# Gated networks of a decoder trunk: two of four weight sums by a transfer that adds, three more block-product pairs in the first network, and another offset for the attention's value weights

## The chip, the cores and the metric

The kernel runs on one core of a Trainium2 chip. The metric is the device time of one execution in microseconds (us), lower is better. It reads HBM through transfers (DMA), works in SBUF, and TensorE (PE) accumulates in PSUM. The other engines are VectorE (DVE), ScalarE (ACT), GpSimd (POOL) and SyncE (SP). Each engine runs its own instructions in order; SP and POOL also issue the transfers here, each in the order of its own queue.

## The reference

Two residual layers over 512 tokens of width 1024 in float32: layer 0 mixes tokens with a state-space block, layer 1 with a forgetting attention of 16 heads, and each is followed by a gated network. Norms are scaled, shifted and gated by adaLN values, which come from products of a conditioning vector with `ada_w`.

```python
def conv_ffn(h, w_up, conv_w, conv_b, w_down):     # h (1, 512, 1024), inner width 2816
    a, b = jnp.split(h @ w_up, 2, axis=-1)
    ap = jnp.pad(a, ((0, 0), (CONV_W - 1, 0), (0, 0)))
    a_conv = conv_b
    for i in range(CONV_W):                        # causal, depthwise, width 3
        a_conv = a_conv + ap[:, i:i + S] * conv_w[i]
    return (jax.nn.silu(a_conv) * b) @ w_down

for i in range(DEPTH):
    h = h + gate * (s5_mixer if i == 0 else fox_mixer)(modulate(h, ...), ...)
    h = h + gate * conv_ffn(modulate(h, ...), ...)
return rmsnorm(h, final_g)
```

## The kernel before

Channels lie on the 128 partitions, the 512 tokens along the free dimension. Every product in question is done in three matmuls: a weight tile and an input are split into a high part (rounded, made by ACT, `w_hi`) and a low part (the rest, made by DVE, `w_lo`), and high x high, high x low and low x high are accumulated (`mms`, L294; `put_parts`, L277 and L278).

**The two networks** (`ffn`). The inner width is 22 tiles of 128. Tile f has a pair of up products, the branch `a` that is convolved and the branch `b` that multiplies it. Inner tiles come in groups: 4, 4, 5, 4, 5 in the first network, 6, 5, 6, 5 in the second. While the pairs of one group are computed, the eight output tiles of the down product of the group before are spread over them, one or two per pair; each is a weight tile of 4 or 5 (second network 5 or 6) blocks of 128 columns. In the first network these down weights are loaded into `rawd`, a room with one buffer, so the second of two tiles can't be loaded until ACT and DVE have read the first. In the second they use `raw`.

**A plain pair** takes two loads of 512 KB (`raw`, three buffers), their parts, and 2 x 8 x 3 matmuls of 512 columns (L294).

**A block-product pair** (`quarters`) takes seven products instead of eight of 4 x 3 matmuls of 256 columns (L550). The weights a11, a12 (branch `a`, upper and lower half of the 1024 inputs), a21, a22 (branch `b`) are combined in four sums s1 to s4 on DVE (L518, tiles `sums`), the inputs in four forms t1 to t4, once per network (`forms_x`, L495). The products are brought together by four combinations on DVE (L518, `nm_t`) from copies that ACT makes of PSUM (L557, `nm_h`). `finish` (`gated`) then makes the two taps (L602) and the gating (L605, L612) and splits the result into `ghi` and `glo`. The list `plain` names the tiles that stay plain; before, 0, 1, 2, 3, 6, 11 and 17 in the first network and 0 to 3 in the second.

**AdaLN sums.** In the first network each tick (one per gated pair after the first group, one after each pair's share of the down product) runs one unit of `ada_units`: DVE multiplies a 512 KB tile with a row and sums it (L247), then POOL's queue loads the next tile into the one buffer `ada_raw` (L233).

**The value weights** of the attention (`fox_values`) are the moving operand of L1366, and lie `VALUES` elements behind the start of their tiles. `aside` does the same for weights of 256-column matmuls, with 22 elements (88 bytes). `fill` only takes up memory.

What each engine does in which order is set by a scheduler that moves instructions of the program by its own estimates; `issue_after` and `behind` restrain it.

Of the kernel before, what the change touches and what calls it, by code (L numbers as in the profile page):

```python
# [8 lines left out]
F32 = mybir.dt.float32  # L9
F32R = mybir.dt.float32r  # L10
I32 = mybir.dt.int32
AF = mybir.ActivationFunctionType
# [5 lines left out]
P = 128  # L18
# [40 lines left out]
def fill(pool, n):  # L59

    pool.tile([P, n // 4], F32, name="fill", bufs=1)


ROOM, ASIDE, VALUES = 9 * P, 22, P - 22


def part_of(pool, shape, name, tag, bufs, aside=0):
# [6 lines left out]
class Trunk:  # L74
# [6 lines left out]
    def __init__(self, tc, io, ctx):  # L81
        self.tc, self.nc, self.io, self.ctx = tc, tc.nc, io, ctx
        nc = self.nc
        pool = lambda name, bufs, **k: ctx.enter_context(tc.tile_pool(name=name, bufs=bufs, **k))
        self.const = pool("const", 1)
        self.act = pool("act", 1)
        self.wpool = pool("wpool", 3)
        self.tmp = pool("tmp", 2)
        self.small = pool("small", 2)
        self.dram = pool("dram", 1, space=DRAM)  # L90
        self.mm = pool("mm", 4, space=PSUM)
        self.aux = pool("aux", 4, space=PSUM)
# [6 lines left out]
        self.room = None  # L99
        self.one = self.const.tile([P, 1], F32, name="one")  # L100
# [11 lines left out]
        fill(self.const, 1728)  # L112
        fill(self.small, 1440 - 1024)

    def load_pack(self, name, parts, pool):
# [360 lines left out]
    def forms_x(self, pool, x):  # L476

        nc = self.nc
        H, N = KT // 2, S // 2
        t1, t2 = HALVES  # L480
        normed = self.last_lo.ins
        b = []
        for j, n in enumerate(("ghi1", "glo1")):
            t = pool.tile([P, H, S], F32, name=f"x{j}", tag=n)
            for c in HALVES:
                k = slice(j * H, (j + 1) * H)
                with self.tc.issue_after(normed):
# [5 lines left out]
        def form(n, u, v):  # L493
            t = pool.tile([P, H, N], F32, name="sums", bufs=2)
            nc.vector.tensor_tensor(t, u, v, ALU.subtract)  # L495
            hi, lo = (pool.tile([P, H, N], F32R, name=m, bufs=4) for m in ("w_hi", "w_lo"))
            self.put_parts(hi, lo, t)
            self.tx[n] = hi, lo
            return t

        f1 = form(1, b[0][:, :, t2], b[0][:, :, t1])
        yield
        f2 = form(2, b[1][:, :, t2], f1)
        yield
        form(4, f2, b[1][:, :, t1])
        yield
        form(3, b[1][:, :, t2], b[0][:, :, t2])
        yield

    def quarters(self, pool, l, f, x, finish):  # L510

        nc = self.nc
        H, N = KT // 2, S // 2
        t1, t2 = HALVES
        a, b = (self.raw([P, KT, P], self.io["w_up"][l][2 * f + j]) for j in range(2))
        a11, a12, a21, a22 = a[:, :H], a[:, H:], b[:, :H], b[:, H:]
        c, d = (pool.tile([P, 2, H, P], F32, name="sums", bufs=2) for _ in range(2))
        sub = lambda o, u, v, op=ALU.subtract: nc.vector.tensor_tensor(o, u, v, op)  # L518
        w = {}
        copied = self.copied  # L520

        def parts(src, names, *where):
            hi, lo = (
                pool.tile([P, H * P + P], F32R, name=n, tag="e" + n)[:, ASIDE:ASIDE + H * P].rearrange("p (n w) -> p n w", w=P)
                if where else part_of(self.wpool, [P, len(names) * H, P], n, n, WB, ASIDE)
                for n in ("w_hi", "w_lo")
            )
            with self.behind(*copied):
                self.put_parts(hi, lo, src)
            for j, n in enumerate(names):  # L530
                w[n] = hi[:, j * H:(j + 1) * H], lo[:, j * H:(j + 1) * H]

        parts(a, ("a11", "a12"))
        sub(c[:, 0], a21, a22, ALU.add)
        sub(c[:, 1], c[:, 0], a11)
        parts(c.rearrange("p n k m -> p (n k) m"), ("s1", "s2"))
        sub(d[:, 1], a11, a21)
        sub(d[:, 0], a12, c[:, 1])
        parts(d.rearrange("p n k m -> p (n k) m"), ("s4", "s3"))
        parts(a22, ("a22",), pool)  # L540
        quarter = lambda k, t: tuple(v[:, k * H:(k + 1) * H, t] for v in x)
        xs = {"b11": quarter(0, t1), "b21": quarter(1, t1), "b22": quarter(1, t2)}
        for n, v in self.tx.items():
            xs[f"t{n}"] = v

        def times(o, wn, xn, first=True):
            (whi, wlo), (xhi, xlo) = w[wn], xs[xn]
            for k in range(H):
                for n, (wt, xt) in enumerate(((whi, xhi), (whi, xlo), (wlo, xhi))):
                    self.last_mm = nc.tensor.matmul(  # L550
                        o, wt[:, k], xt[:, k], start=(first and k == 0 and n == 0), stop=(k == H - 1 and n == 2),
                        skip_group_check=True,
                    )

        def copy(o, last=False):
            t = self.tmp.tile([P, N], F32, name="nm_h", bufs=4)
            a = nc.scalar.activation(t, o, AF.Copy)  # L557
            if last:
                self.copied = [a.ins]
            return t  # L560

        p1, p5 = (self.mm.tile([P, S], F32, name="mmp")[:, :N] for _ in range(2))
        p2, p4 = (self.aux.tile([P, S], F32, name="aux")[:, :N] for _ in range(2))
        oa, ob = (self.tmp.tile([P, S], F32, name="nm_t") for _ in range(2))
        times(p1, "a11", "b11")
        c1 = copy(p1)
        times(p5, "s1", "t1")
        c5 = copy(p5)
        times(p2, "a12", "b21")
        sub(oa[:, t1], p2, c1, ALU.add)  # L570
        times(p1, "s2", "t2", False)
        c2 = copy(p1, True)
        times(p5, "s4", "b22", False)
        sub(oa[:, t2], p5, c2, ALU.add)
        finish(2 * f, oa, slice(0, S))
        times(p4, "a22", "t4")
        c4 = copy(p4)
        times(p1, "s3", "t3", False)
        sub(ob[:, t2], p1, c5, ALU.add)
        sub(ob[:, t1], p1, c4)  # L580
        finish(2 * f + 1, ob, slice(0, S))

    def ffn(self, i, l, x, nxt, ticks=0, plain=None):

        nc, tc = self.nc, self.tc
        with tc.tile_pool(name=f"ffn{l}", bufs=1, reuse_waits="tile") as pool:
            self.bgpool = pool
            conv = pool.tile([P, 4, FT], F32, name="conv_wb")
            nc.sync.dma_start(conv, self.io["conv"][l])
            fill(pool, 1696)  # L590
# [41 lines left out]
            for q, n in enumerate(groups):  # L632
                fs = range(first[q], first[q + 1])
                if not plain:
# [45 lines left out]
class Ew:  # L680
# [29 lines left out]
    def sub(self, a, b, out=None):  # L710
        return self.tt(a, b, ALU.subtract, out)
# [827 lines left out]
def build(tc, io, out, stop=None):  # L1539
    with ExitStack() as ctx:  # L1540
# [105 lines left out]
```

## Time and profile before

| | |
|---|---|
| median of 3 runs | 1214.21 us (1213.31 to 1214.53) |
| profiled execution | 1217.02 us, of which the span of the profile is 1215.2 us |
| clock granted to TensorE, mean | 0.995 |
| DMA | 183.81 MB in 74512 packets, mean 151 GB/s |
| SP's queue / POOL's queue | 161.02 MB, 40.5% / 20.97 MB, 5.4% of 16 engines' span |

All durations below come from the one profiled execution, in us from the start of its span. A row of a group reads: line, engine, operation, output<-inputs, shapes, count, busy us, mean ns of one, and idle time before them with what ended it. A row of the timeline: start, duration, engine, line, operation, count, and in brackets how long the engine had been idle and for whom. A row of a stretch: its limits, its length, then for each engine named the busy time and the number of instructions, the clock granted, the share of the DMA engines and GB/s. A row of waits: who waited for whom, us in total, times, longest. Successive instructions of an engine overlap by some tens of ns, so the distance of starts is what one costs. The lines of the changed kernel are shifted: L277 and L278 become L279 and L280, L518 becomes L533, L550 becomes L563, L602 becomes L614.

### The profile page before, as it was taken

The page shows a single profiled execution, that of the slowest core. Times are in us where ns is not written, and L with a number is a line of the kernel's source. Part 1 is how long each engine was busy: PE and PEld are TensorE (multiplying, and loading weights), DVE is VectorE, ACT ScalarE, POOL GpSimd, SP SyncE. Part 2 cuts the span into 40 slices and gives each one's busy share as a digit, 9 for nine tenths or more (in the row PEclk, how much of TensorE's full clock was granted, in tenths as well). Part 3 has the DMA queues.
Part 4 walks back from the last instruction along what each step waited for, and adds up shares of the span by engine and source line. Part 5 has one row for each costly group of instructions (what it writes and reads, how often), then busy time and mean ns, then how long its engine had stood idle before and what let it go on. Part 6 is the DMA issues. An engine that isn't in the chain of part 4 may idle for free.

```text
span 1215.2 us, 20334 instructions
## 1 busy us (share of the span) xinstructions
PE 1180.3 (97%) x7793; PEld 1015.4 (84%) x7793; DVE 1007.6 (83%) x1872; ACT 609.8 (50%) x1156; POOL 83.9 (7%) x145
## 2 busy tenths in 40 slices
PE   7999999999999999999999999999999999999997
PEld 2566688898989899889899777878989999999987
DVE  7999977789899988898687578875899887888965
ACT  3644555336445454455443565654466554555543
POOL 0000000100000000000000333430000000000000
PEclk9999999999999999999999999999999999999999
DMA  9778786622455544553445543432213332333331
GB/s 348 243 250 261 233 294 220 210 77 70 136 179 164 189 155 148 169 168 106 126 153 180 172 153 130 148 108 88 89 53 113 112 119 90 103 104 109 109 100 70
DMA packets 74512, 183.81 MB, mean 151 GB/s; under 512 B 23231, under 2 KB 25631, under 8 KB 73391
## 3 DMA queue, kind: packets, MB, share of 16 engines
q1 hardware_dynamic: 68367, 161.02, 40.5%
q0 software_dynamic: 5760, 20.97, 5.4%
q8 instruction: 61, 1.00, 0.3%
q10 hardware_dynamic: 288, 0.52, 0.1%
q14 instruction: 36, 0.29, 0.1%
HBM read 175.57 MB, written 6.92 MB: 150 GB/s over the span
## 4 chain that ended last, share of the span: by engine, by line
PE 56%; issue 26%; DVE 8%; DMA 5%; ACT 2%; POOL 2%; SPq 0%; POOLq 0%; DVEq 0%; ACTq 0%
PE mmp L294 24%; PE mmp L550 11%; PE aux L550 4%; PE mmp L1366 3%; PE mmp L1174 2%; DVE w_lo L278 2%; PE mmp L1203 2%; POOL ada_raw L233 1%; PE aux L1505 1%; DMA ada_raw<-in_ada_t 1%; PE aux L1065 1%; PE mmp L1114 1%; PE aux L1057 1%; PE aux L978 1%; DMA yt<-s_yd 1%
## 5 line engine op out<-in xcount | busy, mean ns | idle before, releaser
L278 DVE TENSOR_TENSOR w_lo<-raw,w_hi 128x1024 fp32r<-128x1024 f32 (+4 forms) x173 | 183.3, 1064 | 37.6 <-ACT w_hi L277 31.8
L277 ACT ACTIVATE w_hi<-raw 128x1024 fp32r<-128x1024 f32 (+4 forms) x173 | 154.8, 904 | 105.4 <-PE mmp L294 48.6
L294 PE MATMUL mmp<-ghi,w_hi 128*128 128x512 f32 (+1 forms) x392 | 145.5, 371 | 0.0
L294 PE MATMUL mmp<-ghi,w_lo 128*128 128x512 f32 (+1 forms) x392 | 144.7, 369 | 0.7 <-DVE w_lo L278 0.6
L294 PE MATMUL mmp<-glo,w_hi 128*128 128x512 f32 (+1 forms) x392 | 145.1, 370 | 0.0
L294 PE MATMUL mmp<-a_hi,w_hi 128*128 128x512 f32 (+1 forms) x376 | 138.4, 371 | 1.5 <-ACT a_hi L433 1.5
L294 PE MATMUL mmp<-a_hi,w_lo 128*128 128x512 f32 (+1 forms) x376 | 136.2, 363 | 0.2 <-DVE w_lo L278 0.2
L294 PE MATMUL mmp<-a_lo,w_hi 128*128 128x512 f32 (+1 forms) x376 | 135.7, 362 | 0.0
L550 PE MATMUL mmp<-w_hi 128*128 128x256 f32 x396 | 109.7, 277 | 2.7 <-ACT nm_h L557 2.3
L550 PE MATMUL mmp<-w_hi,w_lo 128*128 128x256 f32 x396 | 109.5, 277 | 0.7 <-DVE w_lo L278 0.7
L550 PE MATMUL mmp<-w_lo,w_hi 128*128 128x256 f32 x396 | 109.4, 276 | 0.0
L557 ACT ACTIVATE nm_h<-mmp 128x256 f32<-128x256 f32 x99 | 37.2, 381 | 107.3 <-PE mmp L550 107.3
L278 DVE TENSOR_TENSOR w_lo<-sums,w_hi 128x1024 fp32r<-128x1024 f32 x74 | 90.0, 1219 | 0.0
L277 ACT ACTIVATE w_hi<-sums 128x1024 fp32r<-128x1024 f32 x74 | 77.0, 1055 | 23.7 <-DVE sums L518 21.7
L294 PEld LDWEIGHTS mmp<-ghi,w_lo 128*128 128x128 f32 x392 | 74.7, 190 | 13.8 <-DVE w_lo L278 1.5
L294 PEld LDWEIGHTS mmp<-ghi,w_hi 128*128 128x128 f32 x392 | 74.7, 191 | 11.5 <-ACT w_hi L277 0.2
L294 PEld LDWEIGHTS mmp<-glo,w_hi 128*128 128x128 f32 x392 | 74.8, 191 | 11.1
L294 PEld LDWEIGHTS mmp<-a_hi,w_hi 128*128 128x128 f32 x376 | 70.2, 188 | 13.8 <-issue 2.6
L294 PEld LDWEIGHTS mmp<-a_hi,w_lo 128*128 128x128 f32 x376 | 70.6, 188 | 12.2 <-DVE w_lo L278 1.2
L294 PEld LDWEIGHTS mmp<-a_lo,w_hi 128*128 128x128 f32 x376 | 70.7, 188 | 9.7
L362 DVE SCALAR_TENSOR_TENSOR h<-mmp,par,h 128x512 f32<-128x512 f32 (+1 forms) x100 | 68.0, 681 | 12.1 <-PE mmp L294 11.9
L550 PEld LDWEIGHTS mmp<-w_hi 128*128 128x128 f32 x396 | 74.3, 188 | 3.2 <-ACT nm_h L557 2.5
(319 smaller groups left out, 3077.7 us busy)
## 6 DMA issues: line engine op xcount, KB each, us to landing
raw<-in_w_up SPq DMA_DIRECT2D x88, 512.0 KB, 3.3
raw<-in_ada_w SPq DMA_DIRECT2D x40, 512.0 KB, 5.6
ada_raw<-in_ada_t POOLq DMA_DIRECT2D x40, 512.0 KB, 3.9
nf<-nfd SPq DMA_DIRECT2D x8, 1152.0 KB, 6.5
raw<-in_fox_qk SPq DMA_DIRECT2D x16, 512.0 KB, 3.7
raw<-in_w_down SPq DMA_DIRECT2D x24, 320.0 KB, 3.1
rawd<-in_w_down SPq DMA_DIRECT2D x24, 256.0 KB, 3.3
raw<-in_w_down SPq DMA_DIRECT2D x16, 384.0 KB, 3.5
```

The source lines that it names most:

```text
L233: (nc.gpsimd if late else nc.sync).dma_start(ws[n], src)
L277: nc.scalar.activation(hi, src, AF.Copy)
L278: return nc.vector.tensor_tensor(lo, src, hi.bitcast(F32), ALU.subtract)
L294: self.last_mm = self.nc.tensor.matmul(o, wt, xt[:, cols], start=(k == 0 and n == 0), stop=(k == nk - 1 and n == 2),)
L362: add = self.nc.vector.scalar_tensor_tensor(self.h[:, m, cols], ps, self.par[i][:, 16 + m:17 + m], self.h[:, m, cols], op0=ALU.mult, op1=A ...
L550: self.last_mm = nc.tensor.matmul(o, wt[:, k], xt[:, k], start=(first and k == 0 and n == 0), stop=(k == H - 1 and n == 2), skip_group_che ...
L557: a = nc.scalar.activation(t, o, AF.Copy)
L978: nc.tensor.matmul(ps[:, :, cols], x[:, q, r].rearrange("p c j -> p (c j)"), both[:, :, planes, q, :], start=(r == 0), stop=(r == 1), skip ...
L1057: nc.tensor.matmul(yp[g2][:, k, :], t[:, g].rearrange("p c i -> p (c i)"), u[:, g, :], start=(k == 0), stop=False, skip_group_check=True,)
L1174: nc.tensor.matmul(ps, w[m][:, k, :], x[:, k], start=(k == 0), stop=(k == KT - 1))
L1203: nc.tensor.matmul(gps[m], wt, xt[:, k], start=(k == 0 and part == 0 and xt is yhi), stop=(k == KT - 1 and part == 1))
L1366: self.last_mm = nc.tensor.matmul(ps[q, b][:, :n], xt[:, k, tb], wt, start=(k == 0 and i == 0), stop=(k == KT - 1 and i == 2),)
```

## The change

1. Two of the four sums come from memory. `pair_sums` loads the first halves of both branches (a11, a21) into a tile `pair` on SP's queue (the base), and then POOL's queue transfers all of branch `b` (a21, a22) onto it with an adding transfer: a11 + a21 and a21 + a22. It is called for tile f + 1 ahead of the work on tile f, with two buffers. `raw` then holds branch `a` (512 KB) and the half a22 (256 KB). The other two sums stay on DVE.
2. Signs are changed so that all four sums are additions: s1 = a21 + a22, s2 = s1 + a11, s3 = a11 + a21, s4 = s2 + a12. Two copies and the second form of the inputs carry a factor -1, and the combinations swap operands.
3. Tiles 6, 11 and 17 of the first network are block products too (15 become 18).
4. `sums` has one buffer instead of two, `pair` has two, and the convolution's weights move from the networks' pools to the constant pool, with fills that keep its size.
5. `VALUES` is 16 elements (64 bytes) instead of 106 (424 bytes).

```diff
-ROOM, ASIDE, VALUES = 9 * P, 22, P - 22
+ROOM, ASIDE, VALUES = 9 * P, 22, 16
...
+        self.conv = self.const.tile([P, 4, FT], F32, name="conv_wb")
+        fill(self.const, 1728 - 16 * FT)
...
-        f1 = form(1, b[0][:, :, t2], b[0][:, :, t1])
+        f1 = form(1, b[0][:, :, t1], b[0][:, :, t2])
-        f2 = form(2, b[1][:, :, t2], f1)
+        f2 = form(2, b[1][:, :, t2], f1, ALU.add, -1.0)
...
+    def pair_sums(self, pool, l, f):
+
+        nc = self.nc
+        H = KT // 2
+        up = self.io["w_up"][l][2 * f:2 * f + 2]
+        t = self.pairs[f] = pool.tile([P, 2, H, P], F32, name="pair", bufs=2)
+        nc.sync.dma_start(t, up[:, :, :H].rearrange("n p k m -> p n k m"))
+        nc.gpsimd.dma_start(t.rearrange("p n k m -> p (n k) m"), up[1], accum_op=ALU.add)
...
-        a, b = (self.raw([P, KT, P], self.io["w_up"][l][2 * f + j]) for j in range(2))
-        a11, a12, a21, a22 = a[:, :H], a[:, H:], b[:, :H], b[:, H:]
-        c, d = (pool.tile([P, 2, H, P], F32, name="sums", bufs=2) for _ in range(2))
+        up = self.io["w_up"][l][2 * f:2 * f + 2]
+        a, a22 = self.raw([P, KT, P], up[0]), self.raw([P, H, P], up[1, :, H:])
+        c, d = self.pairs.pop(f), pool.tile([P, 2, H, P], F32, name="sums", bufs=1)
...
-        sub(c[:, 0], a21, a22, ALU.add)
-        sub(c[:, 1], c[:, 0], a11)
-        parts(c.rearrange("p n k m -> p (n k) m"), ("s1", "s2"))
-        sub(d[:, 1], a11, a21)
-        sub(d[:, 0], a12, c[:, 1])
-        parts(d.rearrange("p n k m -> p (n k) m"), ("s4", "s3"))
+        parts(c.rearrange("p n k m -> p (n k) m"), ("s3", "s1"))
+        sub(d[:, 0], c[:, 1], a[:, :H], ALU.add)
+        sub(d[:, 1], d[:, 0], a[:, H:], ALU.add)
+        parts(d.rearrange("p n k m -> p (n k) m"), ("s2", "s4"))
...
-        c5 = copy(p5)
+        c5 = copy(p5, sign=-1.0)
...
-        c4 = copy(p4)
+        c4 = copy(p4, sign=-1.0)
...
-        sub(ob[:, t2], p1, c5, ALU.add)
-        sub(ob[:, t1], p1, c4)
+        sub(ob[:, t2], c5, p1)
+        sub(ob[:, t1], c4, p1)
...
+                    if f + 1 < FT and f + 1 not in plain:
+                        self.pair_sums(pool, l, f + 1)
...
-        x = k.ffn(1, 0, x, k.norm_mod(2), ticks=1, plain=(0, 1, 2, 3, 6, 11, 17))
+        x = k.ffn(1, 0, x, k.norm_mod(2), ticks=1, plain=(0, 1, 2, 3))
```

The scheduler orders the rest anew. DVE in the first network, tiles 13 to 16, from a pair's first down tile to its second, before (`rawd` is the down weights' room, `raw` the up weights'):

```order
L278 TENSOR_TENSOR w_lo<-rawd,w_hi 128x640
L518 TENSOR_TENSOR sums<-raw 128x512 x2
L518 TENSOR_TENSOR nm_t<-aux,nm_h 128x256
L518 TENSOR_TENSOR sums<-sums,raw 128x512
L518 TENSOR_TENSOR sums<-raw,sums 128x512
L518 TENSOR_TENSOR nm_t<-mmp,nm_h 128x256
L278 TENSOR_TENSOR w_lo<-rawd,w_hi 128x640
```

All four sums of the next pair stood between the two. After, at the same place (tile 14 of the first network):

```order
L280 TENSOR_TENSOR w_lo<-rawd,w_hi 128x640
L533 TENSOR_TENSOR sums<-pair,raw 128x512
L533 TENSOR_TENSOR nm_t<-aux,nm_h 128x256
L533 TENSOR_TENSOR sums<-sums,raw 128x512
L533 TENSOR_TENSOR nm_t<-mmp,nm_h 128x256
L614 SCALAR_TENSOR_TENSOR conv<-nm_t,conv_wb,conv 128x511
L280 TENSOR_TENSOR w_lo<-rawd,w_hi 128x640
```

Two sums and one tap now stand between the two uses of `rawd`. DVE's next rows there, after which come the read of the adaLN sum, `w_lo<-raw,w_hi 128x512` and the next pair's first `rawd` row:

```order
L614 SCALAR_TENSOR_TENSOR conv<-nm_t,conv_wb,conv 128x510
L249 ISA ada_raw,ada_s<-ada_raw,c_row 128x1024
L249 ISA ada_s 128x1
L533 TENSOR_TENSOR nm_t<-nm_h,mmp 128x256 x2
L280 TENSOR_TENSOR w_lo<-raw,w_hi 128x1024
L624 TENSOR_TENSOR conv<-conv,nm_t 128x512
L364 SCALAR_TENSOR_TENSOR h<-mmp,par_93,h 128x512
L280 TENSOR_TENSOR w_lo<-pair,w_hi 128x1024
L280 TENSOR_TENSOR glo<-conv,ghi 128x512
L280 TENSOR_TENSOR w_lo<-sums,w_hi 128x1024
L364 SCALAR_TENSOR_TENSOR h<-mmp,par_93,h 128x512
L249 ISA ada_raw,ada_s<-ada_raw,c_row 128x1024
```

The low parts of `pair` and `sums` now stand with the residuals and the gating. SP's queue at the same tiles, before:

```order
L186 DMA raw<-in_w_up 128x1024 x2
L183 DMA rawd<-in_w_down 128x640 x2
L186 DMA raw<-in_w_up 128x1024 x2
L183 DMA rawd<-in_w_down 128x640 x2
L186 DMA raw<-in_w_up 128x1024 x2
```

and after:

```order
L188 DMA raw<-in_w_up 128x512
L522 DMA pair<-in_w_up 128x2x512
L188 DMA raw<-in_w_up 128x1024
L185 DMA rawd<-in_w_down 128x640 x2
L188 DMA raw<-in_w_up 128x512
L522 DMA pair<-in_w_up 128x2x512
L188 DMA raw<-in_w_up 128x1024
```

The base of the pair after next stands between the half a22 of one pair and the branch `a` of the next. POOL's queue there, before (numbers are buffers):

```order
L233 DMA ada_raw_4912<-in_ada_t 128x1024
L233 DMA ada_raw_4992<-in_ada_t 128x1024
L233 DMA ada_raw_5100<-in_ada_t 128x1024
L233 DMA ada_raw_5182<-in_ada_t 128x1024
L233 DMA ada_raw_5221<-in_ada_t 128x1024
```

and after:

```order
L235 DMA ada_raw_4750<-in_ada_t 128x1024
L523 DMA pair_4940<-in_w_up 128x1024
L235 DMA ada_raw_4858<-in_ada_t 128x1024
L523 DMA pair_5128<-in_w_up 128x1024
L235 DMA ada_raw_4938<-in_ada_t 128x1024
L235 DMA ada_raw_5046<-in_ada_t 128x1024
L523 DMA pair_5318<-in_w_up 128x1024
```

The adding transfers stand between the loads for the adaLN sums.

More of the change, by code (lines that the diff above doesn't have):

```diff
@@ L99, in __init__ @@
         self.room = None
+        self.pairs = {}
         self.one = self.const.tile([P, 1], F32, name="one")
@@ L491, in forms_x, with form @@
         self.tx = {}
-        def form(n, u, v):
-            t = pool.tile([P, H, N], F32, name="sums", bufs=2)
-            nc.vector.tensor_tensor(t, u, v, ALU.subtract)
+        def form(n, u, v, op=ALU.subtract, sign=1.0):
+            t = pool.tile([P, H, N], F32, **(dict(name="pair", bufs=2) if n == 2 else dict(name="sums", bufs=1)))
+            nc.vector.tensor_tensor(t, u, v, op)
             hi, lo = (pool.tile([P, H, N], F32R, name=m, bufs=4) for m in ("w_hi", "w_lo"))
-            self.put_parts(hi, lo, t)
+            if sign < 0:
+                nc.scalar.activation(hi, t, AF.Copy, scale=sign)
+                nc.vector.scalar_tensor_tensor(lo, t, sign, hi.bitcast(F32), op0=ALU.mult, op1=ALU.subtract)
+            else:
+                self.put_parts(hi, lo, t)
             self.tx[n] = hi, lo
             return t
-        f1 = form(1, b[0][:, :, t2], b[0][:, :, t1])
+        f1 = form(1, b[0][:, :, t1], b[0][:, :, t2])
         yield
-        f2 = form(2, b[1][:, :, t2], f1)
+        f2 = form(2, b[1][:, :, t2], f1, ALU.add, -1.0)
         yield
@@ L553, in times, with copy @@
                     )
-        def copy(o, last=False):
+        def copy(o, last=False, sign=1.0):
             t = self.tmp.tile([P, N], F32, name="nm_h", bufs=4)
-            a = nc.scalar.activation(t, o, AF.Copy)
+            a = nc.scalar.activation(t, o, AF.Copy, scale=sign)
             if last:
@@ L587, in ffn @@
             self.bgpool = pool
-            conv = pool.tile([P, 4, FT], F32, name="conv_wb")
+            conv = self.conv
             nc.sync.dma_start(conv, self.io["conv"][l])
-            fill(pool, 1696)
             cw, cb = conv[:, :3], conv[:, 3]
```

1 line of the change is left out of this document (removed).

## The prediction

> **What bounds the kernel now.** I read the page first, then busy time by stretch, the waits of TensorE, and the timeline of the stretch where it waits.
>
> ```profile
> span 1215.2 us, 20334 instructions
> PE 1180.3 (97%) x7793; PEld 1015.4 (84%) x7793; DVE 1007.6 (83%) x1872; ACT 609.8 (50%) x1156; POOL 83.9 (7%) x145
> ...
> 301.20:574.80 273.60, 266.21 (x1789) 242.74 (x1788) 243.81 (x381) 128.80 (x209) 16.40 (x31) 1.00 0.50 159
> 911.20:1167.60 256.40, 256.40 (x1884) 241.55 (x1883) 219.01 (x329) 138.66 (x220) 0.00 (x0) 1.00 0.35 109
> ```
>
> The last two rows are the block-product pairs of the first and of the second network: length, then busy PE, PEld, DVE, ACT, POOL. In the second network PE is busy for all 256.4 us: only fewer matmuls could shorten it, and the change removes none there. In the first PE is idle for 7.4 us and DVE is busy for 243.8 of 273.6. What a matmul costs is read from starts of groups:
>
> ```profile
> 405.62 0.39 PE L294 MATMUL mmp<-a_hi,w_hi 128*128 128x512 f32 x1
> ...
> 416.50 0.39 PE L294 MATMUL mmp<-ghi,w_hi 128*128 128x512 f32 x1
> ...
> 421.94 0.28 PE L550 MATMUL mmp<-a_hi,w_hi 128*128 128x256 f32 x1
> ...
> 431.48 0.40 PE L294 MATMUL mmp<-ghi,w_hi 128*128 128x512 f32 x1
> ...
> 301.20:574.80 273.60, 147.77 (x1259) 146.04 (x1258) 1.00 0.50 159
> 301.20:574.80 273.60, 123.68 (x530) 97.89 (x530) 1.00 0.50 159
> ```
>
> A plain pair's 48 matmuls take 10.88 us (0.2267 each), a block pair's 84 take 9.54 (0.1136 each). The last two rows count L550 and L294 in the first network's stretch: 1259 x 0.1136 + 530 x 0.2267 = 263.2 us of work, so 10.4 of the 273.6 us are lost. Where:
>
> ```profile
> 347.40:359.30 11.90, 9.87 (x86) 1.00 0.55 186
> 486.50:498.50 12.00, 10.36 (x85) 1.00 0.54 177
> 519.40:531.60 12.20, 9.90 (x86) 1.00 0.42 137
> PE mmp L550 <- ACT nm_h L557: 4.3, 2, 2.3
> PE mmp L550 <- DVE w_lo L278: 2.1, 3, 0.9
> ```
>
> Three pairs take 2.4 to 2.7 us more than 9.54 (7.5 together); the rest is in small waits. PE waits for a copy on ACT that is queued behind a weight conversion, or for DVE's low parts: the preparation is late, and this is why:
>
> ```profile
> 440.26 0.82 DVE L278 TENSOR_TENSOR w_lo<-rawd,w_hi 128x640 fp32r<-128x640 f32 x1
> 441.00 0.68 DVE L518 TENSOR_TENSOR sums<-raw 128x512 f32<-128x512 f32 x1
> ...
> 442.54 0.68 DVE L518 TENSOR_TENSOR sums<-raw 128x512 f32<-128x512 f32 x1
> 443.14 0.68 DVE L518 TENSOR_TENSOR sums<-raw,sums 128x512 f32<-128x512 f32 x1
> ...
> 445.93 0.83 DVE L278 TENSOR_TENSOR w_lo<-rawd,w_hi 128x640 fp32r<-128x640 f32 x1 [1.47 <-ACT w_hi L277]
> ...
> 457.70 0.82 DVE L278 TENSOR_TENSOR w_lo<-rawd,w_hi 128x640 fp32r<-128x640 f32 x1
> ...
> 464.12 0.82 DVE L278 TENSOR_TENSOR w_lo<-rawd,w_hi 128x640 fp32r<-128x640 f32 x1 [2.41 <-ACT w_hi L277]
> 475.88 0.81 DVE L278 TENSOR_TENSOR w_lo<-rawd,w_hi 128x640 fp32r<-128x640 f32 x1
> 520.92 0.68 DVE L278 TENSOR_TENSOR w_lo<-rawd,w_hi 128x512 fp32r<-128x512 f32 x1
> 525.68 0.69 DVE L278 TENSOR_TENSOR w_lo<-rawd,w_hi 128x512 fp32r<-128x512 f32 x1
> 457.47 0.53 POOL L233 DMA_DIRECT2D ada_raw<-in_ada_t  x1 [5.74 <-DVE ada_s L247]
> 458.58 6.72 SPq L183 DMA_DIRECT2D rawd<-in_w_down  x2
> 463.34 0.74 ACT L277 ACTIVATE w_hi<-rawd 128x640 fp32r<-128x640 f32 x1 [3.99 <-DMA rawd<-in_w_down]
> ```
>
> `rawd` has one buffer and such a pair needs two tiles, so the second load waits until DVE has read the first: issued at 458.58, used by ACT at 463.34, by DVE at 464.12. From the start of one use to the start of the next (the reload) pass 5.67 and 6.42 us for 640 columns, 4.76 for 512. DVE's round at this stage is 457.70 - 440.26 = 17.4 us, then 18.2; PE's is 9.54 + 30 x 0.2267 = 16.3. DVE falls behind by 1.1 to 1.9 us a pair until PE stops at 486.5.
>
> **The change part by part.** Prices of DVE's work, with the transfers beside it:
>
> ```profile
> L278 DVE TENSOR_TENSOR w_lo<-sums,w_hi 128x1024 fp32r<-128x1024 f32 x74 | 90.0, 1219 | 0.0
> L518 DVE TENSOR_TENSOR nm_t<-mmp,nm_h 128x256 f32<-128x256 f32 x99 | 40.4, 417 | 4.9 <-PE mmp L550 4.9
> L602 DVE SCALAR_TENSOR_TENSOR conv<-nm_t,conv_wb,conv 128x511 f32<-128x511 f32 x33 | 24.6, 746 | 4.9 <-ACT conv L600 4.9
> L247 DVE CUSTOM_DVE_ANT_0 ada_raw<-ada_raw,c_row 128x1024 f32<-128x1024 f32 x40 | 48.6, 1218 | 5.0 <-DMA ada_raw<-in_ada_t 4.8
> raw<-in_w_up SPq DMA_DIRECT2D x88, 512.0 KB, 3.3
> ada_raw<-in_ada_t POOLq DMA_DIRECT2D x40, 512.0 KB, 3.9
> nf<-nfd SPq DMA_DIRECT2D x8, 1152.0 KB, 6.5
> raw<-in_w_down SPq DMA_DIRECT2D x24, 320.0 KB, 3.1
> ```
>
> Instructions overlap by 0.08 us (the sum at 442.54 lasts 0.68, the next starts 0.60 later), so the columns cost 1.14 us for 1024, 0.60 for 512, 0.34 for a 256-wide combination, 0.67 for a tap or a residual, 1.14 for an adaLN sum.
>
> 1. *Three plain pairs become block products.* PE: 3 x (10.88 - 9.54) = 4.0 us less. DVE per pair: low parts of a, c, d and a22, two sums, four combinations (3 x 1.14 + 0.60 + 1.20 + 1.36 = 6.58) instead of two low parts (2.28): 3 x 4.3 = 12.9 us more. ACT gets some 3 us more per pair, at 129 busy of 274: no cost while that idle time is there.
>
> 2. *Two of four sums go.* DVE: 15 old pairs x 2 x 0.60 = 18.0 us less in the first network, so with point 1 it stands at 243.8 - 5.1 = 238.7, against 263.2 - 4.0 = 259.2 on PE. In the second DVE gets 18 x 1.2 = 21.6 us less and PE, never waiting, gains nothing. But in the first a removed sum is no gain where it stood inside a reload: all four sums of the rows above lie between 440.26 and 445.93, where DVE then idles 1.47. So I work out the new round. From the second `rawd` use at this stage to the next pair's first stand, by the new order, the low part (0.74), two taps and two residuals less one tap that lies in the reload (3 x 0.67), two adaLN sums and the low parts of a, pair and sums (5 x 1.14), two combinations (0.68), and three operations of 512 (1.80): 10.9 us, plus a reload of 5.67 to 6.42: 16.6 to 17.3, against PE's 16.3. Behind by 0.3 to 1.0 a pair instead of 1.1 to 1.9. Pairs with two 512-column tiles, by the same count: 0.60 + 4 x 1.14 + 3 x 0.34 + 4 x 0.67 + 3 x 0.60 = 10.7, and 4.76: 15.4 against 9.54 + 24 x 0.2267 = 15.0. With four pairs of each kind DVE still falls 3 to 6 us behind; the other ten are about even (reload covered by 4.8 us and more of other work). I take 5 us lost instead of 10.4: 5.4 us less.
>
> 3. *The adding transfer and its queues.* Per pair the loads grow from 1024 to 1792 KB (512 + 256 raw, 512 base, 512 added). The trace has no adding transfer. Nearest rows: 3.9 us for a plain 512 KB from POOL's queue, 6.5 for 1152 KB; an add also reads what it writes, so I take 6.5, and 13 as the upper end; nothing excludes 3.9. Its cover: the base of a pair is loaded once DVE has read the pair two before, and the sum with it comes about one and a half rounds later, some 22 us: 3.3 + 13 fits. Cost nothing; without that cover every pair in both networks would wait. On SP the base stands between a22 and a of the next pair, and both later loads wait for reads that come no earlier. On POOL an adaLN load now queues behind an add that waits for its base: by the new order the load goes out about 5.3 us after the low part of the pair begins, lands 3.9 later, and the next adaLN sum comes at about 12: some 3 us to spare, also at no cost. Issuing costs POOL 0.53 us, and it idles.
>
> 4. *Value weights at 64 bytes* instead of 424. The attention's L1366 takes 384 matmuls; their pitch beside the block products':
>
> ```profile
> 640.00:650.00 10.00, 10.00 (x85) 10.00 (x85) 1.00 0.76 277
> 912.00:938.00 26.00, 26.00 (x232) 26.00 (x231) 1.00 0.35 114
> 575.00:615.00 40.00, 37.58 (x218) 33.92 (x216) 26.85 (x53) 16.17 (x26) 0.00 (x0) 0.91 0.44 129
> ```
>
> 84 steps in 10.00 us are 0.119 each, 231 in 26.00 are 0.113. If the offset is the reason, 384 x 0.006 = 2.3 us go; if not, nothing. A loss I exclude, as no steady stretch of 256 columns is slower. Neither end is nearer: 1.2. The Trainium skill ("SBUF — State Buffer", section Specifications) states that SBUF has 16-byte lines and each crossing costs; 424 is no multiple of 16 and 64 is, so by that page the whole 2.3 would go and the sum be 1.1 us lower. The trace does not agree fully: the weights of L550 lie at 88 bytes, no multiple either, and run at 0.113.
>
> 5. *conv_wb moves to the constant pool, sign scales on copies*: same instructions and sizes, cost nothing.
>
> Sum against the profiled execution's span: 1215.2 - 4.0 - 5.4 - 1.2 = 1204.6; its own time was 1217.0, so 1206.4. The median of the runs, 1214.2, is 2.8 below that execution: 1203.6.
>
> **Rivals.**
> *The lateness stays* (10.4 us): the reload sets DVE's round and swallows the sums. For it: the sums stood in the reload. Against: the round works out 0.8 us shorter. 1214.2 - 4.0 - 1.2 = 1209.0.
>
> *All lateness goes and the offset works*: 1214.2 - 4.0 - 10.4 - 2.3 = 1197.5. For it: DVE needs 238.7 us against 259.2. Against: the reload is still there.
>
> *Slower: the new transfers lengthen the reload.* Base, add, adaLN load and raw a all go out within about 2 us of the reload of `rawd`. For it: the load issued at 458.58, 1.1 us after an adaLN load, was used 4.76 us later against a median landing of 3.1. Against: transfers take only 0.50 of the engines' time in this stretch. About eleven reloads are not covered, so x us more on each costs 11x: 1203.6 + 11x. From x = 1.2 it is slower; at 1.5 it is 1220. The Trainium skill ("DMA: Bandwidth & Descriptors", section "Issuing engines are not separate DMA queues") speaks for it: transfers of all issuing engines share the same 16 engines, so another queue saves only issue time. By its fitted rate of 436 GB/s (section "Anatomy of one DMA") the 768 KB more are an estimated 1.8 us a pair, which put wholly on the reload gives 1223.
>
> *No change*: the same with x between 0.75 and 1.2.
>
> **How the numbers follow.** Forecast 0.45; lateness stays 0.20; all goes 0.12; no change 0.10; slower 0.13. A measurement of this kernel tells about 0.2% (2.4 us) from no change. Below 1211.8 lie the first three: 0.77. The range from 1197 to 1213 holds these three and the nearer part of the fourth, and leaves out the slower case (0.13) and some 0.05 of edges; the forecast's own is 1201 to 1207 (lateness 3 to 8, offset 0 to 2.3).
>
> **What would show it.** L550 has 36 x 84 = 3024 matmuls instead of 2772, L294 144 fewer. The first network's pairs last 264 us instead of 274; single pairs with 11.9 to 12.2 us become rarer. L518's `sums<-raw` row is replaced by half as many sums with `pair`. The second network's stretch stays at 256. L1366 at 0.113 shows the offset. Wrong it is if DVE waits for `pair` (the adds come late), if the adaLN sums wait for their loads by more than the 4.8 us of now, or if reloads pass 7 us. Outside the sum, the half-clock spell behind the 0.91 in the last row above (575 to 615) may move the time by a few us, since how long PE idles there can shift.

## The result and the profile after

The change made the kernel slower: 1249.33 us (median of 4 runs, 1245.09 to 1256.08) against 1214.37 in the same session, ratio 1.0292, 95% interval 1.0244 to 1.0339. One execution of a run below, e6, was slow at 3035 us, and its ratio leaves it out. The forecast was 1203.6. The profiled execution after took 1256.08 us, at the upper end of its runs and 6.7 us above their median. Its page and two stretches, the first network's block-product pairs and the second's (columns as in the prediction):

```profile
span 1254.0 us, 20731 instructions
PE 1193.5 (95%) x7901; PEld 1026.4 (82%) x7901; DVE 983.1 (78%) x1830; ACT 615.5 (49%) x1174; POOL 114.0 (9%) x181
...
q1 hardware_dynamic: 78159, 170.46, 41.6%
q0 software_dynamic: 10944, 39.85, 13.5%
```

```profile
299.80:615.00 315.20, 281.15 (x1897) 254.96 (x1897) 241.72 (x379) 137.34 (x228) 30.60 (x47) 0.95 0.61 177
950.10:1206.50 256.40, 256.40 (x1885) 241.55 (x1884) 200.55 (x296) 138.66 (x221) 13.59 (x16) 1.00 0.59 157
```

The second network is where it was: PE busy for all 256.4 us. All of the loss lies in the first: 315.2 us for the 259.2 us of work that the prediction counted, so 56.0 lost instead of 10.4. DVE is not the cause by its work: 241.7 us busy, against 243.8 before. Of the 56.0 us PE stands idle for 34.0; in the other 22.0 it is busy for longer than its work. Some 12 of these are a lower clock: the mean of 0.95 is made of seven spells at 0.5, 30.7 us together, and the 96 matmuls that start in them take 12.4 us more than at full clock. The rest, some 10 us, is not put down to a cause here; the kernel before has 3.0 of it at full clock (266.2 busy for 263.2 of work). The block products of one pair show both, idling and a lower clock:

```profile
316.50:335.60 19.10, 11.39 (x85) 10.99 (x84) 12.26 (x21) 6.99 (x13) 1.40 (x2) 0.83 0.54 152
```

The pair takes 19.1 us instead of 9.54, 7.7 of them idle, and its matmuls are busy for 11.39 us; the granted clock is 0.83 on average, so where PE idled this long it also lost clock. What PE waits for late comes from DVE and ACT; what these wait for, in the first network's stretch (who waited for whom, us in total, times, longest):

```profile
ACT w_hi L279 <- DMA rawd<-in_w_down: 68.3, 18, 10.3
DVE w_lo L280 <- ACT w_hi L279: 32.2, 9, 7.0
DVE ada_raw L249 <- DMA ada_raw<-in_ada_t: 25.8, 11, 5.4
PE mmp L563 <- ACT nm_h L570: 14.4, 4, 7.1
```

The same two waits for loads before, in its stretch:

```profile
ACT w_hi L277 <- DMA rawd<-in_w_down: 40.9, 17, 6.1
DVE ada_raw L247 <- DMA ada_raw<-in_ada_t: 0.4, 2, 0.3
```

So two waits have grown, and the timeline shows both. First the round of DVE that the prediction worked out:

```profile
505.51 0.82 DVE L280 TENSOR_TENSOR w_lo<-rawd,w_hi 128x640 fp32r<-128x640 f32 x1
505.66 0.33 SPq L188 DMA_DIRECT2D raw<-in_w_up  x1
505.73 0.87 POOL L523 DMA_DIRECT2D pair<-in_w_up  x1 [7.63 <-DVE w_lo L280]
506.28 0.87 POOL L235 DMA_DIRECT2D ada_raw<-in_ada_t  x1
506.39 10.20 SPq L185 DMA_DIRECT2D rawd<-in_w_down  x2
...
515.41 0.83 DVE L280 TENSOR_TENSOR w_lo<-rawd,w_hi 128x640 fp32r<-128x640 f32 x1 [5.58 <-ACT w_hi L279]
...
526.30 0.82 DVE L280 TENSOR_TENSOR w_lo<-rawd,w_hi 128x640 fp32r<-128x640 f32 x1
```

```profile
506.39 8.17 DMA rawd<-in_w_down
...
514.64 0.74 ACT w_hi L279
...
515.41 0.83 DVE w_lo L280
```

The second fence is the chain at that place: of the work that ended last, followed back, each piece with its start and length. Within 0.9 us after DVE had begun to read `rawd`, four loads go out: branch a, the adding transfer, the next adaLN load, and the reload. The reload is issued at once (506.39, when DVE's read ends), but takes 8.17 us to land. From use to use pass 9.90 us, and the round is 526.30 - 505.51 = 20.8 us. Second, an adaLN sum:

```profile
357.79 1.22 DVE L249 CUSTOM_DVE_ANT_0 ada_raw<-ada_raw,c_row 128x1024 f32<-128x1024 f32 x1
362.31 0.88 POOL L523 DMA_DIRECT2D pair<-in_w_up  x1 [9.99 <-DVE w_lo L280]
362.86 0.88 POOL L235 DMA_DIRECT2D ada_raw<-in_ada_t  x1
369.58 1.23 DVE L249 CUSTOM_DVE_ANT_0 ada_raw<-ada_raw,c_row 128x1024 f32<-128x1024 f32 x1 [5.38 <-DMA ada_raw<-in_ada_t]
```

DVE has done with the tile at 359.0. Its next load stands behind an adding transfer in POOL's queue and goes out at 362.86, 3.9 us late; from there to the sum it takes 6.7 us, where a sum that waited took 3.6 to 3.8 before. DVE idles for 5.38 us.

### The profile page after: what moved, and what is told of

It reads as the page before. It is cut to its first block, busy times and chain, and to the rows that moved or that the text cites. A ratio compares the mean times of both kernels' runs of the same rounds, so it can differ in the third digit from the quotient of the medians.

```text
span 1254.0 us, 20731 instructions
## 1 busy us (share of the span) xinstructions
PE 1193.5 (95%) x7901; PEld 1026.4 (82%) x7901; DVE 983.1 (78%) x1830; ACT 615.5 (49%) x1174; POOL 114.0 (9%) x181
## 3 DMA queue, kind: packets, MB, share of 16 engines
q0 software_dynamic: 10944, 39.85, 13.5%
## 4 chain that ended last, share of the span: by engine, by line
PE 64%; DVE 15%; DMA 12%; ACT 4%; issue 4%; POOL 1%; DVEq 0%; SPq 0%; ACTq 0%; POOLq 0%
PE mmp L296 29%; PE mmp L563 12%; DMA rawd<-in_w_down 5%; DVE w_lo L280 5%; PE aux L563 4%; DMA ada_raw<-in_ada_t 3%; PE mmp L1188 3%; PE mmp L1380 2%; PE mmp L1217 2%; DMA pair<-in_w_up 2%; ACT w_hi L279 1%; PE aux L1079 1%; PE aux L1519 1%; PE aux L1071 1%; PE mmp L207 1%
## 5 line engine op out<-in xcount | busy, mean ns | idle before, releaser
L563 PE MATMUL mmp<-w_hi 128*128 128x256 f32 x432 | 122.3, 283 | 15.1 <-ACT nm_h L570 14.4
L563 PE MATMUL mmp<-w_hi,w_lo 128*128 128x256 f32 x432 | 122.0, 284 | 6.3 <-DVE w_lo L280 6.2
L296 PE MATMUL mmp<-a_hi,w_hi 128*128 128x512 f32 (+1 forms) x328 | 119.6, 368 | 1.5 <-ACT a_hi L435 1.5
L296 PE MATMUL mmp<-a_hi,w_lo 128*128 128x512 f32 (+1 forms) x328 | 117.0, 357 | 0.0
L296 PE MATMUL mmp<-a_lo,w_hi 128*128 128x512 f32 (+1 forms) x328 | 117.0, 357 | 0.0
L563 PEld LDWEIGHTS mmp<-w_hi,w_lo 128*128 128x128 f32 x432 | 83.3, 194 | 7.6 <-DVE w_lo L280 7.5
L563 PEld LDWEIGHTS mmp<-w_lo,w_hi 128*128 128x128 f32 x432 | 83.4, 193 | 0.0
L563 PE MATMUL mmp<-a_hi,w_hi 128*128 128x256 f32 x288 | 80.8, 280 | 0.6 <-ACT w_hi L279 0.6
L563 PE MATMUL mmp<-a_hi,w_lo 128*128 128x256 f32 x288 | 80.6, 280 | 0.8 <-DVE w_lo L280 0.8
L364 DVE SCALAR_TENSOR_TENSOR h<-mmp,par,h 128x512 f32<-128x512 f32 (+1 forms) x100 | 68.1, 683 | 16.3 <-PE mmp L296 16.0
L563 PE MATMUL mmp<-a_lo,w_hi 128*128 128x256 f32 x288 | 80.2, 279 | 0.0
```

The costliest lines, as they stand in the source:

```text
L296: self.last_mm = self.nc.tensor.matmul(o, wt, xt[:, cols], start=(k == 0 and n == 0), stop=(k == nk - 1 and n == 2),)
L364: add = self.nc.vector.scalar_tensor_tensor(self.h[:, m, cols], ps, self.par[i][:, 16 + m:17 + m], self.h[:, m, cols], op0=ALU.mult, op1=A ...
L563: self.last_mm = nc.tensor.matmul(o, wt[:, k], xt[:, k], start=(first and k == 0 and n == 0), stop=(k == H - 1 and n == 2), skip_group_che ...
```

## The experiments

Three questions: is it the adding transfer itself or the bytes it brings (A, B); is it the order of the queues (C); is it the loss of three plain pairs in which DVE caught up (D)? Ratios are to the kernel before in the same session, whose medians were 1214.1 to 1215.6 us. "Lost" is the stretch of the first network's block-product pairs less PE's work (259.2 us with 18 pairs, 263.2 with 15).

**e1, the transfer without the addition.**

```diff
-        nc.gpsimd.dma_start(t.rearrange("p n k m -> p (n k) m"), up[1], accum_op=ALU.add)
+        nc.gpsimd.dma_start(t.rearrange("p n k m -> p (n k) m"), up[1])
```

> The changed kernel with the addition left out of the transfer: the second transfer to `pair` overwrites it with a21 and a22 instead of adding them (so the sums hold the wrong weights); bytes, queues, buffers and the order of every engine are the same. Theory A (the adding transfer itself: its 4 KB packets take 328 ns of an engine in the changed kernel's trace against 159 for plain ones, and packets of `rawd` wait between them): the reload of `rawd`, 9.9 us at tiles 17 to 19, falls to 6 to 7.5, and the time to 1204 + 11 x 1 to 1.5 = 1215 to 1222. Theory B (bytes: 768 KB more per pair at the wrong moment, however they are written): within 1% of 1249. Theory C (order of the queues: the adaLN load stands behind a transfer that waits for its base, SP's loads behind the base): the waits of the adaLN sums, 25.8 us in the first network, stay over 20 us, and the time over 1235.

1226.54 us, ratio 1.0077 (1.0048 to 1.0107). Its stretch, POOL's queue on its page, and two waits of the stretch:

```profile
300.00:589.50 289.50, 273.71 (x1898) 250.09 (x1897) 240.28 (x376) 136.90 (x227) 24.79 (x47) 0.98 0.56 192
...
q0 software_dynamic: 10944, 39.85, 9.3%
...
ACT w_hi L279 <- DMA rawd<-in_w_down: 47.2, 19, 6.6
DVE ada_raw L249 <- DMA ada_raw<-in_ada_t: 11.1, 9, 2.1
```

The same bytes on the same queue cost 9.3% of 16 engines instead of 13.5%, and 25.7 of the 56.0 lost us go (30.3 stay). So the addition itself is about half of the lost time, and 22.8 of the 35.0 us by which the kernel became slower (A), though the time is 4.5 us over the upper end of what A had said. C alone is excluded: the adaLN waits more than halve though no order changed. The rest, 30.3 against 10.4 before, is left to bytes, queue and the plain pairs.

**e2, a second buffer for `rawd`.**

```diff
-ROOM, ASIDE, VALUES = 9 * P, 22, 16
+ROOM, ASIDE, VALUES = 9 * P - 64, 22, 16
...
-            t = self.bgpool.tile(shape, F32, name=self.room, bufs=1)
+            t = self.bgpool.tile(shape, F32, name=self.room, bufs=2 if self.room == "rawd" else 1)
```

> The changed kernel with two buffers for `rawd` (the room comes from the spare columns behind the weight parts, ROOM 64 elements smaller). Nothing else is changed in the program, though the scheduler may move instructions. If the loss is paid in the reload of `rawd` (theories A and B), the transfers may be as slow as they are and the time falls to 1195 to 1210, with DVE's waits for `rawd` under 15 us. If it is paid in the adaLN sums' waits or in SP's queue (theory C), 25 us and more stay: 1225 to 1250.

1220.20 us, ratio 1.0038 (1.0019 to 1.0056): between the two expectations.

```profile
300.50:584.00 283.50, 267.65 (x1897) 249.77 (x1896) 241.04 (x381) 140.13 (x229) 30.68 (x47) 0.99 0.66 197
...
DVE ada_raw L249 <- DMA ada_raw<-in_ada_t: 37.3, 14, 5.3
```

The waits for `rawd` are gone (0.2 us of ACT's are left in the stretch), and lost time falls from 56.0 to 24.3. But the adaLN sums, which had waited 25.8 us, now wait 37.3: with the first wait gone, the second sets the round. C was half right.

**e3, the three pairs alone, all sums on DVE** (the kernel before, with the value weights at 64 bytes).

```diff
-ROOM, ASIDE, VALUES = 9 * P, 22, P - 22
+ROOM, ASIDE, VALUES = 9 * P, 22, 16
...
-        x = k.ffn(1, 0, x, k.norm_mod(2), ticks=1, plain=(0, 1, 2, 3, 6, 11, 17))
+        x = k.ffn(1, 0, x, k.norm_mod(2), ticks=1, plain=(0, 1, 2, 3))
```

> The kernel before with two parts of the change alone: three more block-product pairs in the first network, and the value weights at 64 bytes. All four sums stay on DVE, no transfer adds. Theory A or B (the transfers make the loss): DVE's round of 17.4 to 18.2 us against PE's 16.3 now has no plain pair to catch up in, so lateness grows from 10.4 to 20 us at most: 1214.2 - 4.0 - 1.2 + 3 to 10 = 1212 to 1219. Theory D (the three plain pairs were the slack that kept the first network together): 1235 to 1250, as in the changed kernel.

1221.15 us, ratio 1.0040 (1.0017 to 1.0063), or 1219 on the scale of 1214.2.

```profile
303.90:585.00 281.10, 270.76 (x1896) 247.05 (x1895) 259.28 (x409) 136.66 (x225) 16.37 (x31) 0.99 0.46 155
```

DVE is busy for 259.3 us of 281.1, and 21.9 us are lost. Without plain pairs some 11 us more than before are lost, as A and B had it at their upper end; D, which wanted all 35 us of the slowdown, falls.

**e4, the three tiles plain again.**

```diff
-        x = k.ffn(1, 0, x, k.norm_mod(2), ticks=1, plain=(0, 1, 2, 3))
+        x = k.ffn(1, 0, x, k.norm_mod(2), ticks=1, plain=(0, 1, 2, 3, 6, 11, 17))
```

> The changed kernel with tiles 6, 11 and 17 of the first network plain again: the adding transfers, queues and value weights as changed. Theory A or B: 15 instead of 18 pairs pay, and a plain pair gives DVE 4.3 us to catch up: 1225 to 1240, with reloads of `rawd` still at 8 us and more beside an adding transfer. Theory D: 1205 to 1214.

1234.42 us, ratio 1.0138 (1.0097 to 1.0180).

```profile
300.60:593.60 293.00, 272.62 (x1790) 247.38 (x1789) 228.65 (x355) 131.60 (x211) 27.93 (x44) 0.97 0.61 182
```

29.8 us are lost with DVE busy for only 228.7 us, 15 less than in the kernel before: half the work of the sums was taken from DVE and the kernel became 1.4% slower. The time is in the range of A or B. Still, with these transfers in place the plain pairs matter more than e3 alone says: 56.0 lost us with 18 pairs, 29.8 with 15.

**e5, e2 with the adaLN loads on SP's queue.**

```diff
-                (nc.gpsimd if late else nc.sync).dma_start(ws[n], src)
+                nc.sync.dma_start(ws[n], src)
```

> The changed kernel with two buffers for `rawd` (as in e2, ratio 1.0038) and, besides, the adaLN loads of the first network on SP's queue instead of POOL's. In e2 DVE's waits for `rawd` were gone, and what was left were 37.4 us of adaLN sums waiting for loads that stand behind an adding transfer: held up to 3.2 us on POOL's queue, then 6.0 to 6.5 us to the sum instead of 3.7. Theory A+C (the loss of the change is the reload plus adaLN loads behind the add): these waits fall under 12 us, the first network's pairs from 283.5 to 262 to 270 us, and the time to 1200 to 1208, under the kernel before. Rival B (any 512 KB beside an adding transfer lands in 6 us, whatever its queue; or SP itself is now held): the waits stay over 25 us, somewhere in DVE, and the time at 1215 to 1222.

1198.55 us, ratio 0.9859 (0.9833 to 0.9886): 1.4% faster than the kernel before and 4% faster than the changed one, a little better than A+C had said.

```profile
304.30:564.20 259.90, 259.74 (x1897) 244.17 (x1896) 241.19 (x382) 141.33 (x229) 13.82 (x16) 1.00 0.74 215
...
DVE ada_raw L249 <- DMA ada_raw<-in_ada_t: 4.4, 7, 1.7
```

0.7 us are lost. The adding transfers are still there, as slow as in the changed kernel (median landing 6.7 us against 6.5), and move beside everything else at a DMA share of 0.74: with `rawd` loaded ahead of its use and the adaLN loads out of their queue, they cost next to nothing.

**e8, e2 without the addition** (edits of e1 and e2).

> e2 (two buffers for `rawd`) with the addition left out of the transfer, which overwrites (so the sums hold the wrong weights); the order of every engine is that of e2. It tells what of e2's 37.4 us of adaLN waits is the slow packets of the add and what its place in POOL's queue. Slow packets: the waits fall to 15 us or less and the time to 1203 to 1208. Place in the queue (a load behind a transfer that waits for its base, whatever it does): the waits stay over 25 us, and the time over 1212.

1198.67 us, ratio 0.9868 (0.9833 to 0.9903).

```profile
300.60:564.50 263.90, 261.74 (x1898) 245.89 (x1896) 239.98 (x379) 141.75 (x229) 24.76 (x47) 0.99 0.64 212
...
DVE ada_raw L249 <- DMA ada_raw<-in_ada_t: 16.4, 14, 4.7
```

The place in POOL's queue is that of e2, and 16.4 us of adaLN waits stay, just over the 15 or less expected. But only 4.7 us are lost instead of 24.3, and the time is under the 1203 to 1208 expected. So the queue hurts in the main because what stands ahead in it is slow.

**e10, the adaLN loads on SP alone** (e5's edit on the changed kernel, one `rawd`).

> The changed kernel with the adaLN loads of the first network on SP's queue, and one `rawd` as changed. Theory A+C (two costs that add: the reload of `rawd` beside the add, and the adaLN loads behind it): adaLN waits go from 25.8 us to 10 or less, those for `rawd` stay at 25 to 35 us, and the time falls to 1225 to 1240. Rival (one cost: a single late point that either mends): 1198 to 1206, as with both. Rival (SP now blocks the loads of `rawd`): above 1249.

1240.88 us, ratio 1.0223 (1.0185 to 1.0261), just past the upper end of A+C.

```profile
300.20:602.40 302.20, 278.03 (x1897) 249.39 (x1896) 241.60 (x378) 136.69 (x228) 13.82 (x16) 0.98 0.64 185
...
DVE w_lo L280 <- ACT w_hi L279: 37.9, 12, 6.8
DVE ada_raw L249 <- DMA ada_raw<-in_ada_t: 6.1, 4, 3.5
```

DVE still waits for the high parts of late weights, 37.9 us against 32.2 in the changed kernel. There are two costs, and the `rawd` reload is the larger: from 56.0 lost us the queue alone takes 13.0, the second `rawd` alone 31.7, both 55.3. Since the changed kernel's profiled execution is 6.7 us above its median, each is too large by up to that; by the medians they are 8.5, 29.1 and 50.8 us. The queue alone is hardly clear of noise (1.0185 to 1.0261 against 1.0244 to 1.0339). The costs can't be priced one by one: what e1, e2, e4 and e10 each take away (25.7, 31.7, 26.2 and 13.0 us) is more than the whole.

**e6, a second `rawd` in the kernel before, and e9, the same with the tiles moved.**

```diff
-            t = self.bgpool.tile(shape, F32, name=self.room, bufs=1)
+            t = self.bgpool.tile(shape, F32, name=self.room, bufs=2 if self.room == "rawd" else 1)
...
-            fill(pool, 1696)
+            fill(pool, 1600)     # e6;  e9: 1184
```

> The kernel before with two buffers for `rawd` (the fill of that pool 96 bytes smaller), nothing of the change. If the 10.4 us of lateness in the first network came from the reload of `rawd`, as the prediction had it, DVE's 15.8 us of waits for `rawd` go, its pairs take 264 to 267 us instead of 273.6, and the time is 1204 to 1209. If DVE's work (249 of 279 us) or the adaLN loads set the round, the time stays within 0.3% of before.

> e6 (the kernel before with two buffers for `rawd`) with the fill of that pool at 1184 bytes instead of 1600, so that the tiles behind it lie 512 bytes, not 96, lower than in the kernel before; the order of every engine is that of e6. In e6 PE never stood idle in the first network's pairs, but a pair's 84 matmuls took 9.81 us instead of 9.54 and 24 of the down product 5.61 instead of 5.44. If that is the place of the tiles in memory, the pairs come back to 9.54, the stretch of the first network's pairs to 264 to 266 us (273.6 before), and the time to 1203 to 1208. If it comes with the steady use of PE or with the second buffer, it stays at 9.8 us a pair and 1214 to 1217.

e6: 1216.31 us, ratio 1.0009 (0.9991 to 1.0028). e9: 1202.69 us, ratio 0.9899 (0.9874 to 0.9925). The first network's stretch and one pair's block products, e6 and then e9:

```profile
300.50:570.50 270.00, 270.00 (x1788) 246.63 (x1787) 245.96 (x384) 132.61 (x210) 16.37 (x31) 1.00 0.48 162
...
486.60:496.40 9.80, 9.79 (x84) 9.77 (x83) 1.00 0.57 169
```

```profile
301.20:565.50 264.30, 263.60 (x1788) 242.32 (x1787) 244.65 (x383) 132.43 (x210) 16.44 (x31) 1.00 0.49 164
...
467.40:476.90 9.50, 9.50 (x84) 9.46 (x83) 1.00 0.48 156
```

In both PE hardly idles (0.0 and 0.7 us), so the lateness of the kernel before did come from the reload, as the prediction had read it: in e9 1.1 us are lost instead of 10.4. The time of e6 missed what was expected (1204 to 1209), as it gave the gain back elsewhere: PE is busy throughout at full clock, but 84 matmuls take 9.8 us instead of 9.5. Engine orders are the same in e6 and e9, and the programs differ in the size of the fill alone.

**e7, the value weights alone.**

```diff
-ROOM, ASIDE, VALUES = 9 * P, 22, P - 22
+ROOM, ASIDE, VALUES = 9 * P, 22, 16
```

> The kernel before with the value weights at 64 bytes alone; the order of every engine stays the same. The changed kernel's trace has the 256-column matmuls of that product at a mean pitch of 0.1170 us against 0.1198 before, 384 of them: 1.1 us less, 1213.1, not to be told from no change. If all of them came to 0.1136: 2.4 us less.

1213.99 us, ratio 1.0000 (0.9981 to 1.0019). The stretch that the prediction showed with 85 matmuls of that product:

```profile
640.00:650.00 10.00, 10.00 (x87) 10.00 (x86) 1.00 0.76 283
```

86 steps in 10.00 us are 0.116, not 0.113. Half the effect is there, worth about 1 us, which this measurement can't tell from nothing.

**e11, two `rawd`, three pairs, all sums on DVE** (edits of e9 and e3).

> The kernel before with two buffers for `rawd` (fill as in e9), the three more pairs and the value weights at 64 bytes, all four sums on DVE: e5's network without the adding transfer. In e3 DVE was busy for 264.5 us of the pairs and PE has 259.2 to do, so DVE is the bound: pairs in 265 to 270 us instead of e5's 259.9, time 1203 to 1209. If the adding transfer is worth nothing once `rawd` has two buffers, it comes to e5's 1198.5 within 2 us; if the sums were the loss of e3, it stays above 1212.

1209.88 us, ratio 0.9956 (0.9938 to 0.9973), a little above what was expected.

```profile
300.80:574.10 273.30, 266.11 (x1897) 248.74 (x1896) 260.39 (x412) 139.88 (x228) 16.38 (x31) 0.99 0.46 159
```

14.1 us are lost with DVE busy for 260.4 of 273.3 us (in e3's stretch above it was 259.3, not the 264.5 of the expectation). PE idles for 7.2 us, and 6.9 of them it waits for DVE's low parts: here DVE is the bound. Against e5 that says what the adding transfer is worth once its two side effects are gone, some 11 us with 18 pairs; the two also differ in the adaLN loads' queue and in addresses, which wasn't separated. Against e9, which has none of the change, e5 gains about 0.4%, and the intervals overlap (0.9833 to 0.9886 and 0.9874 to 0.9925), so a gain of the change over a second `rawd` alone is not shown.

## Why the prediction was wrong

**The terms that held.** PE's work fell to 259.2 us as counted, the second network gained nothing, DVE's busy time in the stretch is 241.7 us against the 238.7 forecast. The value weights gave about what was taken (1 us for 1.2), below what can be measured. On SP the base held nothing up at the place above: the load of branch a went out 0.1 us after its buffer's read had ended, and the reload when DVE's read ended. In e5 SP carries the bases and the adaLN loads too, and 0.7 us are lost.

**The step that failed: the reload in the sum of DVE's round.** Term 2 took "10.9 us, plus a reload of 5.67 to 6.42" from the trace of before. The 10.9 was right: 20.8 - 9.90 = 10.9. The reload was not a constant. Over the 14 pairs with two `rawd` tiles the time from one use on DVE to the next was 5.99 us on average before, 8.22 after, and 6.82 in e1, where every engine has the order of the changed kernel: 1.4 of the 2.2 us come with the addition. So the round at the place above became 20.8 us where 16.6 to 17.3 was forecast and PE needs 16.3. This is the rival that was given 0.13. It had the mechanism and put about eleven uncovered reloads at x us each; x was 2.2, which by its formula gives 1203.6 + 24 = 1228, on the slower side. The rest, from 1228 to 1249, is the second step below and the clock. What spoke against the rival, the DMA share of 0.50, was a mean over the stretch: at 505.5 to 506.4 four loads start together, and the share is 0.86 while the reload is under way and 1.01, full, in the 3 us in which most of it passes. The trace of before had it too: 0.84 between 458.6 and 463.3, during the reload that the prediction showed. The rows after:

```profile
506.40:514.60 8.20, 7.17 (x48) 6.21 (x46) 2.55 (x5) 0.82 (x1) 0.74 (x2) 1.00 0.86 232
509.00:512.00 3.00, 3.00 (x19) 2.66 (x19) 0.75 (x1) 0.05 (x1) 0.00 (x0) 1.00 1.01 232
```

**The price of the adding transfer was right, and its place in the argument wrong.** 6.5 us was taken for its landing and 6.5 was its median. "Cost nothing" was said of the wait for `pair`, and DVE indeed hardly waits for it. The cost is what the add does to others. POOL's queue takes 5.4% of 16 engines over 1215.2 us before (65.6 us), 13.5% over 1254.0 after (169.3), 9.3% over 1224.5 in e1 (113.9). The adaLN loads on that queue are the same in all three, so what is above 65.6 us belongs to the 36 new transfers: one that adds takes as much as all 16 engines for 2.9 us, one that overwrites 1.3. The trace's records of single packets say the same: 4 KB take 328 ns with the addition, 159 without (medians).

**The second failed step: "some 3 us to spare" on POOL's queue.** The adaLN load was thought to land 3.9 us after its issue. Ahead of the three longest waits it went out 2.5 to 4.1 us after its tile was free (0.3 before), and then took 6.4 to 7.9 us to the sum, with the slow add ahead of it. That turned 3 us to spare into waits of up to 5.4 us, 25.8 in all. The prediction listed this as a sign of being wrong (adaLN sums that wait by more than the 4.8 us of now), beside reloads over 7 us, which came too, but gave it no rival. e10 prices it at 0.7% of the time beside the reload, hardly clear of noise, and e2 against e5 at 1.8% without the reload.

**The rest of the loss.** That 22.0 of the 56.0 lost us are not idle time, some 12 of them a clock of 0.5, was outside the sum but for one sentence. The clock follows the waits: before, where PE's longest wait in the stretch is 2.3 us, and in e5 it is 1.00, and after, where PE waits for up to 7.1 us, 0.95. The three pairs removed DVE's slack (e3 against before: 11.5 us more lost). Term 2 had set sums taken from DVE against that; that the longer reload undid this is argued from e3, e4 and e5, not separated by a run.

**How the reload grew.** By the trace's packet records the first packet of the reload issued at 506.39 starts 2.8 us later, behind the load of branch a on SP's own queue, as it started 3.1 us after the issue at 458.58 before. But its 128 packets then go out over 4.1 us instead of 1.2. Between 510 and 512 us 77 packets of the add and 72 of `rawd` go out, nearly one for one, where 112 of `rawd` went out in one us with POOL's queue silent (before, from 462 to 463). The Trainium skill ("DMA: Bandwidth & Descriptors", section "Queues, rings and completion order") states that each DMA engine takes turns between the queues that have work, packet by packet. The trace agrees, by the counts above. By that rule a slow packet on one queue is a delay on every other, which the estimate of 1223 by bytes alone missed.

## What to carry to other kernels

A transfer that does arithmetic frees an engine but holds the DMA engines for longer, so its price is paid by whatever load shares its moment, above all one that goes into a single buffer: price the reload with the new neighbours, not with the trace of before, and read the DMA's busy share in the few us where it happens, not over the stage. Give single-buffered rooms that lie in the slower engine's round a second buffer first (here worth 1.0% by itself in e9, though nothing in e6 with other addresses). Keep loads that somebody waits for out of a queue in which slow transfers stand. With both done (e5) the slow transfers cost next to nothing here; with the buffer alone (e2) 24.3 us stayed lost.

## What the hardware showed that was not expected

An adding transfer of 512 KB took 2.2 times the DMA engines' time of the same transfer without addition (2.9 against 1.3 us of all 16 engines), though its median landing rose only from 4.4 (e1) to 6.5 us.

The place of tiles in memory moved the pitch of matmuls by 3%: with the fill 96 bytes smaller than before (e6) a block product's 84 matmuls took 9.8 us, with the fill 512 bytes smaller (e9) 9.5, at the same order of every engine and full granted clock. In the whole kernel that was 1.1%. The rule of 16-byte lines in the Trainium skill ("SBUF — State Buffer", section Specifications), by which each crossing into a new line costs, does not explain it, since the two differ by 416 bytes, a multiple of 16; what does was not tried.
